# One transformer layer on one Trainium2 core: operand halves, k's pieces, norm scales and the first feed-forward weights made a step earlier at the joints between stages

## The chip, the cores and the metric

One core of one Trainium2 chip. TensorE (PE) multiplies, VectorE (DVE), ScalarE (ACT) and GpSimd (POOL) work on tiles in SBUF and PSUM, and SyncE (SP), POOL and ACT issue transfers. The metric is the time of one execution on the device in microseconds (us); lower is better.

## The reference

One layer on x of 1024 rows by 1024 columns, fp32, with three blocks, each between two RMS norms (`pre` before, `post` after, on the residual):

```python
h = swiglu(rmsnorm(x, ffn1_pre_g), wg1, wu1, wd1)        # 1024 -> 2816 -> 1024
x = x + 0.5 * rmsnorm(h, ffn1_post_g)
qkv = rmsnorm(x, mix_pre_g) @ w_qkv                      # 16 heads of 64
o_na  = neighbourhood_attention(heads 0..7)              # 2-D windows of a 16 x 64 grid
o_dil = dilated_mixture_attention(heads 8..15)           # windows (128,1) (512,4) (2048,16)
x = x + rmsnorm(concat(rmsnorm(o_na), rmsnorm(o_dil)) @ w_out, mix_post_g)
h = swiglu(rmsnorm(x, ffn2_pre_g), wg2, wu2, wd2)
x = x + 0.5 * rmsnorm(h, ffn2_post_g)
# swiglu(x, g, u, d) = (silu(x @ g) * (x @ u)) @ d
```

## The kernel before, in words

**Products.** Every fp32 operand is split into a high part (rounded to fp32r by ACT, names `whi`, `x`) and the remainder (DVE, `wlo`), and a product is three matmuls (`mm3`, L317 to L319). Gate, up, q, k and the down products go by the seven products of Strassen and Winograd over halves of 512 rows and columns. A left operand (`Operand`) therefore has quadrants A11, A12, A22 and sums S1 to S4; a right one (`PairGemm` for pairs such as gate and up of one block of 128 columns, or q and k) has B11, B22 and T1, T2.

**Operand.** The normed x comes in eight tiles of 128 rows. Tiles 0 to 3 are transposed on PE (`trp`, L157), split into A11 and A12, and a raw copy is saved to DRAM. Tile t from 4 on fetches the saved half of tile t-4 (`early_half`, L212, queue of POOL, shown as `x<-xn`) and forms the sums from it and from its own two transposes: `left_half`, `right_half`, with steps for S2, S1, S3 and at last S4 (`end`, L272), which the turns take one by one from a list. Where `c.deep` is 1 (the operands of q, k, v and of the second feed-forward; there `c.xn` is 0 and the norm is written in place) the fetched half has one place, tag `x1`.

**PairGemm.** `ahead` makes the A11 and A12 products of the first pairs (10 in the second feed-forward) while the operand's later tiles are still being made: a turn is two chains of four `mm3`, 24 matmuls. `start` fetches the first two weights (`graw`), `split_left(b)` splits weight b and fetches b+2. `run` then makes the rest of each pair: u2, v (L548, `v<-mmp,u`), c22 (L567), and in `last`, one turn later, c21 (L575, `c<-mmp,u`), the split of B22 and the fetch of the weights two pairs on. A sink takes the finished quarters: `GatePairs` for gate and up, `QKPairs` for q and k, which splits a piece (ACT L930, DVE L931, both named `qk`) and writes it to DRAM (L936 to L942; a strip is 128 by 8 by 64).

**Attention.** Eight dilated heads, then eight neighbourhood heads. Scores `sp` (L1051), their sums `sa` (L972), `q` and `g` sorted by residue on POOL (L961), probabilities transposed (`ptp`), copied (`pt`, L984), then `po`. Output goes to `og`. `GroupNorm` squares on ACT (L1213), makes 1/rms by a chain of small DVE operations (L131 to L143), scales `og` (L1220) and transposes it (L1231) as the operand of the out projection, whose turns `plan` fills with the next operand's steps: `fin.scale` and `rest` (L788), `U(t)` puts tile t, `G(t)` fetches a row block.

**Order.** `order` inside `ordered()` and the lists `todo`, `steps` and `sums` set which step is recorded in which turn; PE goes in the order in which the code is written, and a scheduler sorts the other engines' instructions by priority. Each engine and each queue runs in order. `nat_chain` products (`accp`) are the out projection's.

**Tail.** `Finish(...)` closes the second feed-forward: in `half` ACT squares a half of the product (L150) and DVE multiplies it by the gain in place (L750); `end` makes 1/rms (L128 to L143) and adds to the residual (L767).

## Time and profile before

| | us |
|---|---|
| median of 3 runs | 1929.8 (1928.88 to 1931.73) |
| the profiled execution | 1927.83 |
| its span, first to last instruction | 1926.0 |
| PE busy | 1851.6 (96%) |
| DVE busy | 1325.9 (69%) |
| ACT busy | 832.0 (43%) |
| POOL busy | 319.9 (17%) |
| mean granted clock of TensorE | 0.988 |

A row of a timeline has start and length in us, engine, line, operation, output from inputs, and in brackets the idle time of the engine just before and what ended it. A row of the waits has the engine's instruction, what it waited for, the total in us, how often, and the longest. The stages follow one another: first feed-forward to 690, q, k, v to 947 (the QK run from 840), attention to 1185, out projection to 1264, the second feed-forward's ahead phase to 1335, its run to 1700, the down products to 1915, tail to 1926.

### The profile page before, as it was taken

How to read it: one execution, taken by the hardware profiler on the slowest of the kernel's cores; microseconds unless marked ns; L12 is line 12 of the kernel's file. 1: busy time of each engine (PE TensorE's matmuls, PEld its weight loads, DVE VectorE, ACT ScalarE, POOL GpSimd, SP SyncE). 2: the span in 40 equal slices, each digit the busy share in tenths (PEclk: the TensorE clock that was granted, in tenths of full speed). 3: DMA queues.
4: the chain of work that ended last, by engine and by line, in shares of the span. 5: the costliest groups of instructions: out<-in, count | busy, mean ns of one | idle time of the engine just before them, and what ended most of it. 6: DMA issues, size and time to landing. Idle time of an engine off the chain costs nothing.

```text
span 1926.0 us, 25147 instructions
## 1 busy us (share of the span) xinstructions
PE 1851.6 (96%) x8904; PEld 1536.5 (80%) x8904; DVE 1325.9 (69%) x2233; ACT 832.0 (43%) x1491; POOL 319.9 (17%) x504
## 2 busy tenths in 40 slices
PE   7899999999999989998899998999999999999997
PEld 6787888888778867877799997877888888888886
DVE  6777776765565875556677765777788777654557
ACT  7422333333344555223488765455222333344332
POOL 2123211111030122122433100121111111110000
PEclk9999999999999999999999999999999999999999
DMA  7656565547886757556968540575456655476563
GB/s 270 211 169 207 204 225 211 195 164 248 295 306 216 269 187 257 193 178 221 299 224 259 170 142 23 190 280 186 158 192 238 216 193 210 159 267 216 200 227 136
DMA packets 169296, 404.95 MB, mean 210 GB/s; under 512 B 17793, under 2 KB 40225, under 8 KB 167122
## 3 DMA queue, kind: packets, MB, share of 16 engines
q1 hardware_dynamic: 121330, 242.66, 37.9%
q0 software_dynamic: 46832, 158.59, 22.9%
q10 hardware_dynamic: 1008, 2.10, 0.3%
q8 instruction: 70, 1.15, 0.2%
q14 instruction: 56, 0.46, 0.1%
HBM read 277.34 MB, written 130.99 MB: 212 GB/s over the span
## 4 chain that ended last, share of the span: by engine, by line
PE 47%; issue 27%; DMA 9%; DVE 9%; POOL 3%; ACT 3%; SPq 1%; DVEq 0%; POOLq 0%; ACTq 0%
PE mmp L319 9%; PE mmp L317 9%; PE mmp L318 9%; PE accp L318 4%; PE accp L319 4%; PE accp L317 4%; PE po L1072 2%; PE ptp L982 2%; DMA wraw<-in_wqk_dram 2%; PE po L1184 2%; DMA wraw<-in_wu_dram 1%; DVE pw L674 1%; DMA tsv<-tr 1%; PE sp L1051 1%; DVE wlo L414 1%
## 5 line engine op out<-in xcount | busy, mean ns | idle before, releaser
L317 PE MATMUL mmp<-x,whi 128*128 128x512 f32 (+1 forms) x1464 | 581.4, 397 | 19.4 <-DVE v L548 10.9
L319 PE MATMUL mmp<-x,wlo 128*128 128x512 f32 (+1 forms) x1464 | 577.5, 394 | 3.9 <-DVE wlo L414 3.9
L318 PE MATMUL mmp<-x,whi 128*128 128x512 f32 (+1 forms) x1464 | 575.7, 393 | 1.3 <-DVE x L240 0.8
L317 PEld LDWEIGHTS mmp<-x,whi 128*128 128x128 f32 x1464 | 278.2, 190 | 84.7 <-ACT whi L413 10.0
L319 PEld LDWEIGHTS mmp<-x,wlo 128*128 128x128 f32 x1464 | 277.9, 190 | 68.6 <-DVE wlo L414 5.9
L318 PEld LDWEIGHTS mmp<-x,whi 128*128 128x128 f32 x1464 | 278.3, 190 | 62.6 <-DVE x L240 1.1
L674 DVE TENSOR_TENSOR pw<-praw,pw 128x1024 fp32r<-128x1024 f32 (+1 forms) x181 | 199.7, 1148 | 115.7 <-ACT pw L673 115.3
L673 ACT CAST pw<-praw 128x1024 fp32r<-128x1024 f32 (+1 forms) x181 | 168.6, 982 | 208.3 <-PE accp L319 150.3
L318 PE MATMUL accp<-pw 128*128 128x512 f32 x600 | 234.4, 391 | 5.9 <-DVE pw L674 5.6
L317 PE MATMUL accp<-pw 128*128 128x512 f32 x600 | 234.8, 391 | 0.3 <-DVE hb L730 0.2
L319 PE MATMUL accp<-pw 128*128 128x512 f32 x600 | 233.6, 389 | 0.0
L413 ACT CAST whi<-wraw 128x1024 fp32r<-128x1024 f32 x129 | 135.3, 1051 | 219.1 <-PE mmp L318 184.5
L414 DVE TENSOR_TENSOR wlo<-wraw,whi 128x1024 fp32r<-128x1024 f32 x129 | 158.2, 1228 | 19.9 <-ACT whi L413 19.7
L318 PEld LDWEIGHTS accp<-pw 128*128 128x128 f32 x600 | 112.7, 188 | 31.6 <-DVE pw L674 9.0
L317 PEld LDWEIGHTS accp<-pw 128*128 128x128 f32 x600 | 112.7, 188 | 25.1 <-ACT pw L673 1.2
L319 PEld LDWEIGHTS accp<-pw 128*128 128x128 f32 x600 | 112.6, 188 | 23.3
L621 POOL DMA_DIRECT2D g<-sg x44 | 23.9, 544 | 471.1 <-DVE sg L614 296.4
L413 ACT CAST whi<-traw 128x512 fp32r<-128x512 f32 x52 | 32.4, 623 | 152.3 <-DVE traw L503 95.6
L502 DVE TENSOR_TENSOR wraw<-wraw 128x1024 f32<-128x1024 f32 x52 | 63.7, 1225 | 45.4 <-DMA wraw<-in_wqk_dram 26.2
L432 ACT COPY s<-mmp 128x512 f32<-128x512 f32 x52 | 30.6, 588 | 139.4 <-PE mmp L319 136.4
L575 DVE TENSOR_TENSOR c<-mmp,u 128x512 f32<-128x512 f32 x52 | 35.9, 690 | 76.9 <-PE mmp L319 76.8
L1184 PE MATMUL po<-vs,pt 128*128 128x128 f32 x352 | 50.3, 276 | 2.0 <-ACT pt L984 1.7
(278 smaller groups left out, 2761.1 us busy)
## 6 DMA issues: line engine op xcount, KB each, us to landing
praw<-g SPq DMA_DIRECT2D x70, 512.0 KB, 6.0
wraw<-in_wg_dram SPq DMA_DIRECT2D x44, 512.0 KB, 4.2
wraw<-in_wu_dram SPq DMA_DIRECT2D x44, 512.0 KB, 6.2
tr<-in_wd_dram SPq DMA_DIRECT2D x44, 512.0 KB, 6.5
g<-sg POOLq DMA_DIRECT2D x88, 256.0 KB, 4.1
ts<-tr POOLq DMA_DIRECT2D x22, 1024.0 KB, 4.8
praw<-ts SPq DMA_DIRECT2D x88, 256.0 KB, 4.3
praw<-in_wd_dram SPq DMA_DIRECT2D x66, 256.0 KB, 4.9
```

Source lines behind the costliest of these rows:

```text
L317: nc.tensor.matmul(out, ahi, bhi, start=start, stop=False, skip_group_check=go_on)
L318: nc.tensor.matmul(out, ahi, blo, start=False, stop=False, skip_group_check=go_on)
L319: nc.tensor.matmul(out, alo, bhi, start=False, stop=stop, skip_group_check=go_on)
L413: nc.scalar.copy(hi, raw)
L414: nc.vector.tensor_sub(lo, raw, hi.bitcast(F32))
L502: nc.vector.tensor_sub(r[:, 0:2], r[:, 1:3], r[:, 0:2])
L575: nc.vector.tensor_add(c21, d, u2)
L673: nc.scalar.copy(hi, raw[:, :m])
L674: nc.vector.tensor_sub(lo, raw[:, :m], hi.bitcast(F32))
L982: nc.tensor.transpose(ps[:, j, :], src[:, j * P:(j + 1) * P], c.ident)
L1072: nc.tensor.matmul(po[:, un * 2 + j], pt[:, 2 * j + t, :], rhs, start=t == 0, stop=t == 1)
L1184: nc.tensor.matmul(po[0][:, u], pt[0][:, j, :], vs[:, k0 + j, :], start=j == 0, stop=j == n - 1)
```

## The change

1. Operands with `c.xn` 0: the saved halves of tiles 5 and 7 are fetched as soon as tile 4's and tile 5's second transposes are recorded, into places of tag `x`; that of tile 6 at the end of tile 4, into `x1`.
2. `run` hands c22 to the sink right away (`third`); `QKPairs` puts k's second half there and no longer in `last`. The last pair's strips go by SP's queue.
3. End of attention: the squares of `most` and with them the norm of the first quad are recorded a turn sooner.
4. The second feed-forward's first weights are fetched at turn 6 of the out projection rather than 8, and weight 0 is split at its turn 10. Every third weight of the ahead phase, from 0 on, has a place of its own (`p0`), the others share two instead of three.
5. Tiles 6 and 7 of the second feed-forward's operand are put in turns 5 and 6 rather than 6 and 7.
6. In the tail the gain's product for the last four tiles goes to a tile `hm` of its own.

```diff
         self.parts[t] = deque(((A11, xn[:, :T]), (A12, xn[:, T:])))
-        if t >= 4:
+        if t == 4 or t > 4 and c.xn:
             self.early_half(t)
...
         c = self.c
-        x1 = self.half[t] = c.xp.tile([P, 2, 4, P], F32, tag="x1", name="x1", bufs=c.deep)
+        if t % 2 and not c.xn:
+            x1 = c.xp.tile([P, D], F32, tag="x", name="x1", bufs=c.xbufs).rearrange("p (i k x) -> p i k x", i=2, k=4)
+        else:
+            x1 = c.xp.tile([P, 2, 4, P], F32, tag="x1", name="x1", bufs=c.deep)
+        self.half[t] = x1
         c.nc.gpsimd.dma_start(x1, self.saved[t - 4].rearrange("p i (k x) -> p i k x", k=4))
...
             self.open -= 1
+            if t == 4 and not c.xn:
+                self.early_half(6)
         a22 = transposed(c, src)
+        if t in (4, 5) and not c.xn:
+            self.early_half(2 * t - 3)
         add(s1, a21, a22)
...
             nc.vector.tensor_add(c22, d, v)
+            self.sink.third(b, c22)
             sums()
...
 
+    def third(self, b, up):
+        pass
+
     def last(self, b, gate, up):
...
 
-    def __init__(self, c, src, dst, gain, op):
-        self.c, self.src, self.dst, self.gain, self.op = c, src, dst, gain, op
+    def __init__(self, c, src, dst, gain, op, last=False):
+        self.c, self.src, self.dst, self.gain, self.op, self.last = c, src, dst, gain, op, last
         self.ss = c.small.tile([P, 8, 2], F32, tag="fss", name="fss", bufs=1)
...
         sumsq(self.c, h, self.ss[:, t, g:g + 1])
-        self.c.nc.vector.tensor_mul(h, h, self.gain[:, g * T:(g + 1) * T])
+        to = h
+        if self.last and t >= 4 and g == 0:
+            to = self.part = self.c.xp.tile([P, T], F32, tag="hm", name="hm")
+        self.c.nc.vector.tensor_mul(to, h, self.gain[:, g * T:(g + 1) * T])
 
...
             sl = slice(g * T, g * T + T)
-            nc.vector.scalar_tensor_tensor(x[:, sl], h[:, sl], r, x[:, sl], op0=ALU.mult, op1=ALU.add)
+            nc.vector.scalar_tensor_tensor(x[:, sl], h[:, sl] if g else self.part, r, x[:, sl], op0=ALU.mult, op1=ALU.add)
             queue.dma_start(self.dst[t][:, sl], x[:, sl])
...
 
+    def third(self, b, k):
+        self.put(b, 1, 1, k)
+
     def last(self, b, q, k):
         self.put(b, 0, 1, q)
-        self.put(b, 1, 1, k)
 
...
                 dst = d[:, j].rearrange("p (s x) -> p s x", s=8)[:, :, h * 64:h * 64 + 64]
-                nc.gpsimd.dma_start(dst, e[:, j].bitcast(F32).rearrange("p (s x) -> p s x", s=8))
+                (nc.sync if h and b == 7 else nc.gpsimd).dma_start(dst, e[:, j].bitcast(F32).rearrange("p (s x) -> p s x", s=8))
         else:
...
             e = sub()
-            early_pools(e)
+            early_pools(e, 2 if pg.own else 3)
             if begin:
...
             c.pw, c.pr, c.ha, c.tj = pool("pw", 5, w), pool("pr", 4, w), pool("ha", 1, w), pool("tj", 1, m)
-            fin = Finish(c, src, dst, load_gain(c, post, "post"), None)
+            fin = Finish(c, src, dst, load_gain(c, post, "post"), None, pre is None)
             hs = {}
...
                     c.todo.append(lambda n=n, i=i: c.behind(lambda: n.squares(slice(0, 448), 0, (i, i + 1)), ACT))
+            c.tick()
         with ordered():
...
                     if (p, hd) == (NP - 1, 1):
-                        c.todo.extend([lambda: None, most])
+                        c.todo.append(most)
                     na_head(c, p, hd, og[0], vs, st, nb, next_ready, last if (p, hd) == (NP - 1, 1) else lambda q: None)
...
             pg = gate_pairs(3, op, a["wg2"], a["wu2"], 10)
+            pg.own = pool("p0", 1, prep, side="right")
             fin = Finish(c, x1, x2, p2, op)
...
                         c.behind(c.w.split, DVE, ACT)
-            plan(12, {0: [lambda: fin.scale(0, 4), A(0, 1)], 2: [A(2, 3)], 5: [U(0)], 6: [U(1)], 7: [G(4)],
-                      8: [lambda: queued(pg.start), G(5)], 9: [U(2)], 10: [U(3)], 11: [G(6)]})
+            plan(12, {0: [lambda: fin.scale(0, 4), A(0, 1)], 2: [A(2, 3)], 5: [U(0)], 6: [U(1), lambda: queued(pg.start)], 7: [G(4)],
+                      8: [G(5)], 9: [U(2)], 10: [U(3), lambda: pg.split_left(0)], 11: [G(6)]})
             for t in range(4):
...
             ffn(3, op, prep, pg, get2,
-                {0: [G(7), lambda: fin.scale(4, 4), A(4, 5)], 1: [A(6, 7)], 3: [U(4)], 4: [U(5)], 6: [U(6)], 7: [U(7)]},
+                {0: [G(7), lambda: fin.scale(4, 4), A(4, 5)], 1: [A(6, 7)], 3: [U(4)], 4: [U(5)], 5: [U(6)], 6: [U(7)]},
                 down_sums(a["wd2"], ts2), [], a["ffn2_post_g"], None, x2, o)
```

At the start of attention POOL's queue stood as follows before; `qk` are pieces of q and k on their way to DRAM, `st` and `q` the first head's operands, `g` its bias:

```order
251 L942 DMA qk_1_75<-qk 256x1x512
252 L961 COPY g<-g 128x384
253 L940 DMA qk_0_74<-qk 128x8x64 x2
254 L942 DMA qk_1_75<-qk 256x1x512
255 L942 DMA qk_1_77<-qk 256x1x512
256 L952 DMA st<-qk_0_78 128x1024
257 L961 COPY g<-g 128x384
258 L940 DMA qk_0_76<-qk 128x8x64 x2
259 L942 DMA qk_1_77<-qk 256x1x512
260 L961 COPY q<-st 128x1024
```

The same place after the change (L957, L959, L969, L978 are the former L940, L942, L952, L961):

```order
244 L957 DMA qk_0_72<-qk 128x8x64 x2
245 L959 DMA qk_1_75<-qk 256x1x512 x2
246 L978 COPY g<-g 128x384
247 L957 DMA qk_0_74<-qk 128x8x64 x2
248 L959 DMA qk_1_77<-qk 256x1x512 x2
249 L969 DMA st<-qk_0_78 128x1024
250 L978 COPY g<-g 128x384
251 L978 COPY q<-st 128x1024
```

The last pair's strips and pieces (`qk_0_76`, `qk_1_77`), which stood between the second `g` and `q`, are gone from between them: the strips to SP, the pieces of k ahead of `st` and that `g`.

On POOL, too, the second feed-forward's saved halves, `x_...<-xn_1` to `xn_3`, stood among the saves of the ahead phase's products (`s1d`, `sgd`), one per tile:

```order
330 L212 DMA x_11363<-xn_1_10688 128x1024
331 L487 DMA s1d<-s_11554 128x512
332 L604 DMA sgd<-sg 128x512
333 L487 DMA s1d<-s_11604 128x512
334 L212 DMA x_11439<-xn_2_10689 128x1024
335 L604 DMA sgd<-sg 128x512
336 L487 DMA s1d<-s_11656 128x512
337 L604 DMA sgd<-sg 128x512
338 L212 DMA x_11448<-xn_3_10690 128x1024
```

and now:

```order
318 L613 DMA sgd<-sg 128x512
319 L216 DMA x_11482<-xn_1_10688 128x1024
320 L495 DMA s1d<-s_11488 128x512
321 L613 DMA sgd<-sg 128x512
322 L216 DMA x_11531<-xn_2_10689 128x1024
323 L216 DMA x_11551<-xn_3_10690 128x1024
324 L495 DMA s1d<-s_11557 128x512
325 L613 DMA sgd<-sg 128x512
```

The fetches of the last two tiles now follow that of tile 5 after two saves, next to each other (L216, L495, L613 are the former L212, L487, L604).

On DVE the first of the second feed-forward's `wlo<-graw` stood in pair with the second before:

```order
1497 L240 TENSOR_TENSOR x_10686<-raw,x_10685 128x4x128
1498 L134 TENSOR_SCALAR y<-v 128x4
1499 L135 TENSOR_SCALAR y<-y 128x4
1500 L141 TENSOR_TENSOR e<-y,v 128x4
1501 L414 TENSOR_TENSOR wlo<-graw,whi 128x1024 x2
1502 L142 TENSOR_TENSOR e<-e,y 128x4
1503 L143 SCALAR_TENSOR_TENSOR y<-e,y 128x4
```

and stands now in the out projection, among the small operations of the pre-norm's scale (L133 to L143) and the products by the gain (L1790):

```order
1454 L133 TENSOR_SCALAR v<-ss 128x2
1455 L1790 TENSOR_TENSOR hs<-accp,gain 128x512
1456 L134 TENSOR_SCALAR y<-v 128x2
1457 L1790 TENSOR_TENSOR hs<-accp,gain 128x512
1458 L135 TENSOR_SCALAR y<-y 128x2
1459 L422 TENSOR_TENSOR wlo<-graw,whi 128x1024
1460 L141 TENSOR_TENSOR e<-y,v 128x2
1461 L142 TENSOR_TENSOR e<-e,y 128x2
```


The first weight's low part (L422 is the former L414) moved out of the phase that needs it into the stage ahead; the second stays where the pair was.

## The prediction

> **What bounds the kernel now.** I read the page's busy shares first, then the waits of TensorE (PE) summed by releaser, then the windows and the timelines around the longest of these waits. The first fence has the page's busy line and then windows (span, length, busy time of PE, PEld, DVE, ACT, POOL, granted clock, DMA share, GB/s).
>
> ```profile
> PE 1851.6 (96%) x8904; PEld 1536.5 (80%) x8904; DVE 1325.9 (69%) x2233; ACT 832.0 (43%) x1491; POOL 319.9 (17%) x504
> 720.00:730.00 10.00, 6.91 (x24) 5.33 (x23) 4.46 (x6) 3.05 (x5) 1.72 (x3) 0.83 0.63 215
> 855.00:865.00 10.00, 7.21 (x33) 5.67 (x32) 7.74 (x10) 4.14 (x5) 4.61 (x7) 1.00 0.81 222
> 950.00:960.00 10.00, 7.80 (x41) 7.32 (x41) 4.57 (x24) 7.44 (x23) 6.09 (x5) 0.66 1.06 344
> 1185.00:1195.00 10.00, 7.51 (x32) 5.64 (x32) 7.57 (x32) 3.67 (x16) 0.00 (x0) 0.83 0.00 0
> 1264.00:1335.00 71.00, 64.87 (x280) 50.40 (x278) 56.08 (x99) 41.84 (x70) 15.63 (x29) 0.95 0.69 238
> 1265.00:1275.00 10.00, 7.78 (x20) 5.73 (x21) 8.32 (x20) 4.82 (x8) 2.09 (x4) 0.66 0.67 226
> 1334.00:1344.00 10.00, 9.66 (x34) 7.55 (x35) 6.65 (x9) 3.29 (x5) 0.54 (x1) 0.83 0.91 322
> 1335.00:1700.00 365.00, 365.00 (x1584) 298.24 (x1584) 271.77 (x342) 114.11 (x150) 47.27 (x83) 1.00 0.56 194
> ```
>
> PE is busy 96% of the span, and in the long run of the second feed-forward (1335 to 1700) all of it: 365.00 us for 1584 matmuls is 0.230 us each, so a turn of 24 matmuls there lasts 5.5 us. No edit removes a matmul, so only time in which PE stands still or runs at a lower clock can be won. The joints between stages have both. A window of 10 us at clock 0.83 loses 10 x 0.17 = 1.7 us, one at 0.66 loses 3.4.
>
> The waits of PE by releaser (total, times, longest) name the places:
>
> ```profile
> PE mmp L317 <- DVE v L548: 10.9, 7, 2.8
> PE mmp L317 <- ACT whi L413: 4.4, 2, 2.3
> PE mmp L319 <- DVE wlo L414: 3.9, 3, 3.1
> PE sp L1051 <- DVE sa L972: 2.9, 1, 2.9
> PE trp L1231 <- DVE og L1220: 2.5, 1, 2.5
> PE sp L1051 <- POOL q L961: 1.7, 1, 1.7
> ```
>
> **The change, part by part.**
>
> *Operand of q, k, v (term a).* The fetch of a tile's saved half (L212) waited for the one place of x1, which comes free at the previous tile's last subtraction (L272). For tiles 5 and 7 it now goes to a place of x right behind the transposes, for tile 6 right behind tile 4's end. DVE around the wait of 3.1:
>
> ```profile
> 717.88 0.69 DVE L278 TENSOR_TENSOR s<-s,x 128x512 f32<-128x512 f32 x1 [0.82 <-DMA x<-xn]
> 722.10 2.35 DVE L414 TENSOR_TENSOR wlo<-graw,whi 128x1024 fp32r<-128x1024 f32 x2
> 723.37 0.50 PE L319 MATMUL mmp<-x,wlo 128*128 128x512 f32 x1 [3.09 <-DVE wlo L414]
> ```
>
> DVE stood 0.82 for that fetch, and the wlo that PE needs stands behind all of tile 5's subtractions. In the new order one wlo goes ahead of two of them (2 x 0.69) and the 0.82 is gone: 2.2 of the 3.09. Ends: 0.8 (the 0.82 alone) and 3.1. New issues on POOL cost nothing on the path: POOL is 17% busy.
>
> *k's second half a step sooner (term b).* In seven turns of the QK run PE waits for v, 10.9 in all.
>
> ```profile
> 859.82 1.08 DVE L931 TENSOR_TENSOR qk<-c,qk 128x512 fp32r<-128x512 f32 x1 [0.33 <-ACT qk L930]
> 870.08 1.23 DVE L502 TENSOR_TENSOR wraw<-wraw 128x1024 f32<-128x1024 f32 x1 [6.64 <-DMA wraw<-in_wqk_dram]
> ```
>
> At 859.82 k's subtraction stands ahead of v; it moves behind it, 0.33 + 1.08 = 1.4 sooner. But the next turn starts with weights whose landing DVE already awaits for 6.64, so that turn gives most of it back. I take 1.0; ends 0 and 2.
>
> *Start of attention (term c).* The last pair's subtraction for k and its DMAs stood between PE's last matmul and the first scores; the strips go to SP.
>
> ```profile
> 947.98 1.08 DVE L931 TENSOR_TENSOR qk<-c,qk 128x512 fp32r<-128x512 f32 x1 [1.25 <-ACT qk L930]
> 948.98 0.68 DVE L931 TENSOR_TENSOR qk<-qk 128x512 fp32r<-128x512 f32 x1
> 948.76 0.91 POOL L940 DMA_DIRECT2D qk<-qk  x1 [0.27 <-ACT qk L930]
> 949.96 0.89 POOL L940 DMA_DIRECT2D qk<-qk  x1 [0.28 <-DVE qk L931]
> 950.84 0.70 POOL L942 DMA_DIRECT2D qk<-qk  x1
> 951.42 2.13 POOL L961 CAST q<-st 128x1024 fp32r<-128x1024 f32 x1
> ```
>
> One subtraction goes ahead of the others, about 1.0 off the wait of 2.9 for the scores' sums; the other (948.98) stays. POOL's cast of q stood behind three issues (0.91 + 0.89 + 0.70 with waits between, 2.7): without them it ends sooner than PE needs it, and the wait of 1.7 goes. Sum 2.7; ends 1.0 (q then waits for the landing of st) and 4.6 (both waits whole). What SP gets is two issues ahead of the first loads of v, needed only after the scores.
>
> *End of attention (term d).* The chain of twelve small operations that makes the scale, from the second row to the third, ran behind the last og; it now stands ahead, in the 2.28 in which DVE idled.
>
> ```profile
> 1184.10 0.42 DVE L1192 TENSOR_TENSOR og<-po,rd 128x256 f32<-128x256 f32 x1 [2.28 <-PE po L1184]
> 1184.44 0.15 DVE L131 TENSOR_TENSOR v<-gss 128x4 f32<-128x4 f32 x1
> 1187.02 2.08 DVE L1220 SCALAR_TENSOR_TENSOR og<-og,y,gd 128x512 f32<-128x512 f32 x3
> 1175.44 0.56 ACT L1213 ACTIVATE junk<-og 128x448 bf16<-128x448 f32 x1
> ```
>
> 1187.02 - 1184.44 = 2.6 less before the transpose: the whole wait of 2.5. Against it, squares such as that of 0.56 on ACT now stand among the copies that PE awaits; I charge one. 2.0; ends 0 (four of them are paid) and 2.5.
>
> *First weights of the second feed-forward (term e).* ACT and DVE made them after the out projection, where nothing covered them:
>
> ```profile
> 1265.92 2.01 ACT L413 CAST whi<-graw 128x1024 fp32r<-128x1024 f32 x2
> 1267.16 2.36 DVE L414 TENSOR_TENSOR wlo<-graw,whi 128x1024 fp32r<-128x1024 f32 x2
> ```
>
> The first split now stands some 25 us earlier, beside the out projection's matmuls. What goes is the wait for whi, 2.3, and 0.2 more for wlo: 2.5. If that cover is gone (DVE is dense there) the piece costs 1.0 + 1.2 where it is put, and 0.3 is left: ends 0.3 and 2.5. The two new places of weights keep a rotation of three, so no later weight is fetched later.
>
> *Tiles 6 and 7 a turn sooner, halves fetched early (term f).*
>
> ```profile
> 1307.90 0.69 DVE L278 TENSOR_TENSOR s<-s,x 128x512 f32<-128x512 f32 x1 [2.82 <-DMA x<-xn]
> 1331.70 1.22 DVE L502 TENSOR_TENSOR wraw<-wraw 128x1024 f32<-128x1024 f32 x1
> L269 DVE TENSOR_TENSOR x<-s,x 128x512 fp32r<-128x512 f32 x16 | 10.7, 687 | 1.5 <-ACT x L268 1.4
> L414 DVE TENSOR_TENSOR wlo<-graw,whi 128x1024 fp32r<-128x1024 f32 x10 | 12.1, 1222 | 1.4 <-ACT whi L413 1.4
> ```
>
> At the phase's end PE waits 2.1 (4.4 less 2.3) for whi, since DVE comes to the run's first weights only at 1331.70; 0.6 more is left of the waits for wlo (3.9 - 3.1 - 0.2). DVE's 2.82 for the fetch goes, and the tiles come 5.5 sooner, so DVE is there before PE. 2.5; ends 0 and 2.7.
>
> *Tail (term g).* Four tiles run in a chain on DVE; the gain's product waits for ACT's square, which reads the same tile:
>
> ```profile
> 1901.33 0.69 DVE L733 TENSOR_TENSOR hb<-accp,hb 128x512 f32<-128x512 f32 x1 [2.81 <-PE accp L319]
> 1915.18 0.39 PE L319 MATMUL accp<-pw 128*128 128x512 f32 x1
> 1917.50 0.69 DVE L733 TENSOR_TENSOR hb<-accp,hb 128x512 f32<-128x512 f32 x1
> 1919.03 0.69 DVE L750 TENSOR_TENSOR hb<-hb,gain 128x512 f32<-128x512 f32 x1 [0.85 <-ACT junk L150]
> ```
>
> From 1901.33 to 1917.50 is three tiles, 5.39 each, against PE's 4.75: the first add starts as its matmuls end, and the last matmul is out at 1915.57, 14.2 later. With a tile of its own the product fills the 0.85, and the scale starts when ACT's sum is in, 0.6 sooner per tile. 5.39 - 0.6 = 4.8, about PE's own pace: the last tile starts 1.8 sooner and ends 0.6 sooner still, 2.4. Ends 0.6 and 2.5.
>
> *Clock (term h).* Windows at 0.83 or 0.66 stand behind five of the waits: q, k, v 1.7, start of attention 3.4, its end 1.7, first weights 3.4, end of the phase 1.7, in all 11.9. The tie isn't strict: 855 to 865 holds the longest wait for v, 2.8, and shows 1.00. I count half of the four whose wait goes (8.5), so 4.2, and nothing at the start of attention, where a wait of 1.9 stays; ends 0 and 11.9. [...]
>
> Sum: 2.2 + 1.0 + 2.7 + 2.0 + 2.5 + 2.5 + 2.4 + 4.2 = 19.5. The profiled execution took 1927.83 (span 1926.0 and 1.83 around it), which gives 1908.3; the median of the runs lies 1.97 above it, so the forecast is 1910.
>
> **The rivals.** [...]
>
> *The feed-forward's joint gives nothing* (e = f = 0): the split is paid in the out projection, and DVE, now fed four tiles in four turns, is as late at the end as before. Left are 2.2 + 1.0 + 2.7 + 2.0 + 2.4 = 10.3 and half of 3.4 of clock (terms a and d), 12.0: 1918.
>
> *Other waits in the same places:* landings end each joint instead of the queues; only g's 2.4 stay, 1927. Against it speaks that in a, d, e, g the last releaser is an engine.
>
> *DVE becomes the bound and the kernel is slower.* A tile takes nine operations of 0.687 (L276, L278, L279, L272 and five of L269), 6.2, and the turn's weight 1.22: 7.4 against PE's 5.5. With tiles 4 to 7 in consecutive turns DVE falls back 1.9 in each; if wlo is queued behind the tiles, PE waits four times 1.9, 7.6, and each wait draws 1.7 of clock: 14.4 lost, against 10.3 won elsewhere: 1929.8 + 4.1 = 1934. For it: DVE is busy 56.08 of 71 us there. Against: 15 us are idle, the 2.82 goes, and wlo is ordered ahead of some tile steps. It decides once the losses of the phase pass what the other joints save, 10.3.
>
> **How the numbers follow.** Forecast 0.46, clock as it is 0.22, joint without gain 0.18, other waits 0.06, DVE bound 0.08. The range takes in the first three with their bounds: all low ends and no clock would be 2.7 off, all high ends 31.8 off, both unlikely, so 1901 to 1925. Some 0.2% (3.9 us) is what a measurement of this kernel can tell from no change: faster 0.86, same 0.06, slower 0.08.
>
> **What would show it.** Right: the waits named og L1220, POOL q and ACT whi L413 missing from PE's list; wlo at the q, k, v joint under 0.6; the last hb add at about 0.2 behind PE's last matmul; clock 1.00 in the windows behind. Wrong: waits of PE for wlo or x between the feed-forward's turns, or a second low window there; DVE waiting for graw or x1 landings; L548 waits still at 10.

## The result

The changed kernel ran at 1917.24 us (median of 4, 1916.26 to 1917.54) beside 1930.76 for the kernel before: ratio 0.9947, interval 0.993 to 0.9964. Run twice more beside before, it came to 0.9940 (0.9928 to 0.9952) and 0.9941 (0.9925 to 0.9956). So it is 0.5 to 0.6% faster, 11 to 13.5 us by the medians; the forecast was 20.

The page after, and the waits of TensorE (total, times, longest) over the whole span, as they answer to those before:

```profile
span 1915.8 us, 25139 instructions
PE 1846.7 (96%) x8904; PEld 1535.6 (80%) x8904; DVE 1328.6 (69%) x2233; ACT 832.6 (43%) x1491; POOL 318.2 (17%) x502
PE mmp L325 <- DVE v L556: 7.2, 4, 3.4
PE trp L157 <- DVE x L204: 5.8, 1, 5.8
PE sp L1068 <- DVE sa L989: 3.5, 1, 3.5
PE accp L325 <- DVE hb L742: 1.9, 1, 1.9
PE mmp L327 <- DVE wlo L422: 0.9, 2, 0.5
PE trp L1248 <- DVE og L1237: 0.7, 1, 0.7
```

(L325 to L327 are the former L317 to L319, L421 and L422 the former L413 and L414, L273 the former L269.) The waits that an edit aimed at are down or gone: og from 2.5 to 0.7, q from POOL gone, wlo at q, k, v from 3.1 to 0.4 (the other 0.5 of its row lies in the second feed-forward). That for sa has grown from 2.9 to 3.5, and one for hb is new.

To see where the time went I matched one DVE instruction per stage in the traces. Each number is how much longer a stage took than in the profiled execution of before (us; minus is faster). The stages end at: the add of the thirteenth hb (679.4 in before), the first k (834.4), the last k (943.3), the first neighbourhood head's og (1080.7), the last hs (1265.1), the run's last c (1705.6), the last pass's first hb (1884.5), the end.

| kernel | first feed-forward | q, k, v | QK run | attention start | its end, out projection | 2nd feed-forward | down | tail | all |
|---|---|---|---|---|---|---|---|---|---|
| forecast, with half of the clock | 0 | -3.1 | -1.0 | -2.7 | -2.9 | -7.6 | 0 | -2.4 | -19.5 |
| changed | +1.8 | -3.6 | +0.1 | -1.9 | -4.4 | -3.4 | +1.8 | -0.5 | -10.3 |
| again | +2.1 | -3.1 | +0.9 | -2.0 | -4.4 | -1.8 | +0.4 | -2.0 | -9.9 |
| again2 | +0.2 | -2.6 | -1.3 | -2.0 | -4.5 | -3.7 | +0.6 | -2.1 | -15.4 |
| no_halves | +2.8 | -0.7 | +2.9 | -1.1 | -3.1 | +1.1 | +1.2 | -2.0 | +1.0 |
| no_turn67 | -0.3 | -2.3 | -0.4 | -1.6 | -4.4 | -3.9 | +0.1 | -2.1 | -14.9 |
| no_first | -0.1 | -3.8 | +1.0 | -1.2 | -4.3 | -3.1 | +0.5 | -2.0 | -13.1 |
| no_qk | +0.9 | -4.8 | +0.5 | -1.0 | -4.4 | -3.5 | +0.3 | -2.4 | -14.6 |
| no_most | +1.7 | -1.3 | +1.3 | -1.8 | -1.8 | -2.0 | +1.9 | -0.6 | -2.5 |
| no_tail | +1.0 | -3.9 | -0.7 | -2.0 | -4.5 | -3.3 | +2.0 | +0.4 | -11.0 |
| sp7 | +0.6 | -2.6 | -1.0 | -2.0 | -4.4 | -4.0 | +1.3 | -2.1 | -14.2 |
| order_fix | -0.0 | -3.6 | -1.4 | -2.0 | -4.4 | -5.0 | +0.4 | -2.0 | -18.0 |
| order2 | +0.6 | -2.8 | +3.1 | -1.9 | -3.1 | -4.0 | +0.2 | -1.1 | -8.9 |
| q_on_act | -0.2 | -4.1 | +1.1 | -2.5 | -4.5 | -1.8 | +0.1 | -2.0 | -13.9 |
| joined | -1.4 | -2.7 | -0.7 | -2.7 | -3.1 | -4.8 | -0.2 | -2.1 | -17.7 |
| joined2 | -0.7 | -2.8 | +2.3 | -2.7 | -4.4 | -6.5 | -0.1 | -2.1 | -17.1 |
| joined3 | +3.2 | -3.4 | -0.7 | -2.5 | -3.1 | -5.3 | -0.2 | -2.1 | -14.0 |
| warm | +6.7 | -0.8 | +1.6 | -1.8 | -4.5 | -2.0 | -0.8 | -1.7 | -3.4 |
| warm_joined2 | +5.4 | -3.1 | +4.0 | -2.6 | -3.1 | -6.5 | -0.7 | -2.0 | -8.6 |
| pick | +2.7 | -3.1 | -1.0 | -0.4 | -4.4 | -6.1 | +0.0 | -2.5 | -14.8 |

The first feed-forward and the QK run scatter by 4 to 5 us from one execution to the next, in kernels that are alike there; the start of attention repeats within about 1. The tail is at about -2; changed and no_most show less because a stretch of half clock in the last pass cost them 1.5, order2 because its end came 1.0 later, and no_tail has the edit undone. The largest gap against the forecast is the second feed-forward: 7.6 was expected, 1.8 to 3.7 came in three executions.

TensorE's clock splits these three. The traces record stretches of half clock, 3.4 us or a multiple long (3.41 and 6.83 at 0.50 in that of the changed kernel, from 876.25 and 947.93). Changed and again2 have none in this phase (-3.4, -3.7), again has one of 3.4 (-1.8). Five more kernels have the same code there: no_tail and no_qk without a stretch are at -3.3 and -3.5, no_most, q_on_act and warm with one at -1.8 to -2.0. One stretch is therefore worth about 1.6 in this column, and runs are best compared with others that have as many.

Waits of TensorE in that phase alone, before (1258 to 1340) and after (1250 to 1332):

```profile
PE mmp L317 <- ACT whi L413: 4.4, 2, 2.3
PE mmp L317 <- ACT s L432: 0.8, 1, 0.8
PE mmp L319 <- DVE wlo L414: 0.8, 2, 0.6
```

```profile
PE trp L157 <- DVE x L273: 2.6, 2, 1.8
PE mmp L325 <- ACT whi L421: 1.5, 1, 1.5
PE mmp L325 <- ACT raw L238: 1.4, 1, 1.4
PE trp L157 <- ACT s L260: 1.3, 1, 1.3
PE mmp L327 <- DVE wlo L422: 0.5, 1, 0.5
```

Before they come to 6.0, after to 7.3. Not one microsecond of waiting was won there: the first weights' wait passed to the copy that frees a PSUM bank (raw, 1.4), and three waits of the transposes are new. What was won is clock. In before 1264 to 1335 had 0.95; after, the same phase has:

```profile
1256.00:1326.00 70.00, 63.75 (x289) 50.35 (x287) 56.94 (x102) 41.70 (x69) 16.18 (x30) 1.00 0.72 256
```

The two low windows of before there (0.66 from 1265, 0.83 from 1334) had lost 3.4 and 1.7, together 5.1; 5.1 of clock won and 1.3 more waiting make 3.8, about the 3.4 measured.

Why the transposes wait stands on DVE and POOL (timelines of the changed kernel):

```profile
1269.84 0.55 POOL L613 DMA_DIRECT2D sgd<-sg  x1 [2.46 <-ACT sg L609]
1270.37 0.55 POOL L495 DMA_DIRECT2D s1d<-s  x1
1270.91 0.54 POOL L804 DMA_DIRECT2D x<-x  x1
1280.90 1.28 DVE L204 SCALAR_TENSOR_TENSOR x<-x,y,gain 128x1024 f32<-128x1024 f32 x1 [2.75 <-DMA x<-x]
1284.16 1.23 DVE L510 TENSOR_TENSOR wraw<-wraw 128x1024 f32<-128x1024 f32 x1 [0.84 <-DMA wraw<-in_wu_dram]
1285.30 0.68 DVE L284 TENSOR_TENSOR s<-s,trp 128x512 f32<-128x512 f32 x1
1324.93 0.62 ACT L421 CAST whi<-traw 128x512 fp32r<-128x512 f32 x1 [1.96 <-PE mmp L326]
```

Row block 7 is stored to DRAM and then normalised in place (L204), so DVE has to see the store read. The changed order put that store on POOL behind a product's `sgd`, which waits for ACT. It was issued 3.2 after DVE had made the block and landed 9.4 after its issue had ended, and DVE stood 2.75. Then it stood for L510, a sum of the second pair's weights, taken far ahead of its use. Tile 4 begins only behind both. And at the run's start ACT took the second pair's T2 (`traw`), whose place TensorE was still reading, ahead of the first pair's T1, for which TensorE then waited.

### The profile page after: what moved, and what is told of

It reads as the page before. It is cut to its first block, busy times and chain, and to the rows that moved or that the text cites. A ratio compares the mean times of both kernels' runs of the same rounds, so it can differ in the third digit from the quotient of the medians.

```text
span 1915.8 us, 25139 instructions
## 1 busy us (share of the span) xinstructions
PE 1846.7 (96%) x8904; PEld 1535.6 (80%) x8904; DVE 1328.6 (69%) x2233; ACT 832.6 (43%) x1491; POOL 318.2 (17%) x502
## 5 line engine op out<-in xcount | busy, mean ns | idle before, releaser
L325 PE MATMUL mmp<-x,whi 128*128 128x512 f32 (+1 forms) x1464 | 580.3, 396 | 15.9 <-DVE v L556 7.2
L327 PE MATMUL mmp<-x,wlo 128*128 128x512 f32 (+1 forms) x1464 | 576.9, 394 | 0.9 <-DVE wlo L422 0.9
L325 PEld LDWEIGHTS mmp<-x,whi 128*128 128x128 f32 x1464 | 278.0, 190 | 79.9 <-issue 5.1
L327 PEld LDWEIGHTS mmp<-x,wlo 128*128 128x128 f32 x1464 | 277.7, 190 | 64.2 <-DVE wlo L422 2.2
L325 PE MATMUL accp<-pw 128*128 128x512 f32 x600 | 235.6, 393 | 2.4 <-DVE hb L742 1.9
L421 ACT CAST whi<-wraw 128x1024 fp32r<-128x1024 f32 x129 | 135.3, 1051 | 231.6 <-PE mmp L326 211.5
L327 PE MATMUL accp<-pw 128*128 128x512 f32 x600 | 234.4, 391 | 0.0
L422 DVE TENSOR_TENSOR wlo<-wraw,whi 128x1024 fp32r<-128x1024 f32 x129 | 158.2, 1229 | 19.9 <-ACT whi L421 19.8
L325 PEld LDWEIGHTS accp<-pw 128*128 128x128 f32 x600 | 113.0, 188 | 27.2 <-issue 2.3
L327 PEld LDWEIGHTS accp<-pw 128*128 128x128 f32 x600 | 113.1, 189 | 23.5
L421 ACT CAST whi<-traw 128x512 fp32r<-128x512 f32 x52 | 32.3, 622 | 141.2 <-DVE traw L511 76.0
L510 DVE TENSOR_TENSOR wraw<-wraw 128x1024 f32<-128x1024 f32 x52 | 63.7, 1224 | 35.5 <-DMA wraw<-in_wqk_dram 25.3
L575 DVE TENSOR_TENSOR c<-mmp,v 128x512 f32<-128x512 f32 x52 | 35.9, 690 | 25.1 <-PE mmp L327 24.6
```

What stands on the lines that cost most here:

```text
L325: nc.tensor.matmul(out, ahi, bhi, start=start, stop=False, skip_group_check=go_on)
L327: nc.tensor.matmul(out, alo, bhi, start=False, stop=stop, skip_group_check=go_on)
L421: nc.scalar.copy(hi, raw)
L422: nc.vector.tensor_sub(lo, raw, hi.bitcast(F32))
L510: nc.vector.tensor_sub(r[:, 0:2], r[:, 1:3], r[:, 0:2])
L575: nc.vector.tensor_add(c22, d, v)
```

## The experiments

**The parts undone, one at a time.** The change's own kernel once more:

> The changed kernel once more, unaltered. If the profiled execution of it was typical, the ratio to before is 0.993 to 0.996 again, the second feed-forward's waits of transposes (1.4, 2.0 and 0.9) stand in the new trace at the same places, and the wait of 1.9 for hb in the down products either stands again (then the change causes it) or is gone (then it was one execution's landing).

0.9940 of before. The transposes' waits stood at the same places (1.28, 1.83 and 0.75 of idle time, some 0.17 less than the expectation's way of counting from matmul to matmul). The wait for hb was 0.5. It comes to 1.4 to 2.2 in no_halves, no_most, no_tail and sp7 as well, where, as in changed, DVE stood 7.6 to 8.8 for a row block of the residual (5.3 in before); the down products took 1.2 to 2.0 longer in these five. In again2, where DVE stood 8.0, it is 0.8. So it comes and goes with a landing that varies between executions; whether the change has a part in it is not shown.

```diff
-                {... 5: [U(6)], 6: [U(7)]},
+                {... 6: [U(6)], 7: [U(7)]},
```

> The changed kernel with tiles 6 and 7 of the second feed-forward put in turns 6 and 7 again, all else kept. If DVE is what sets the ahead phase (four tiles in a row at 7.4 against PE's 5.5), the waits of transposes shrink by about 2 to 3 and as much comes back at the phase's end: no change within 1.5 against the changed kernel. If putting them sooner was worth the 2.5 of the forecast, this is 2.5 slower than the changed kernel. If it costs, this is 2 to 3 faster.

0.9929 (0.9916 to 0.9942), the phase at -3.9. The waits of transposes go, those of 0.4 and 2.0 ahead of the run come back, and the phase's waits sum to 5.8, not 7.3. Putting the tiles a turn sooner is worth nothing; if anything it costs, since this execution has one stretch of half clock in the phase and the changed order with one is at -1.8 to -2.0.

```diff
-            pg.own = pool("p0", 1, prep, side="right")
-            ... 6: [U(1), lambda: queued(pg.start)] ... 10: [U(3), lambda: pg.split_left(0)]
+            ... 6: [U(1)] ... 8: [lambda: queued(pg.start), G(5)] ... 10: [U(3)]
```

> The changed kernel with the first weights fetched and split where they were before (and the three shared places). If the split in the out projection was worth the forecast 2.5, this is 2.5 slower, and up to 6 with the low clock behind it. If the wait at the phase's start only passes to the copy that frees a PSUM bank (1.4 in the changed kernel's trace), 1 slower. If DVE sets the phase, the start is later by 1 to 2 and the transposes' waits shrink by as much: no change.

0.9951 (0.9937 to 0.9964), the phase at -3.1, inside the scatter of the changed kernel (-1.8 to -3.7). The start waits 2.3 and 0.7 again; the transposes' waits fall from 3.9 to 3.0 and the run's start has none. The phase's waits sum to 6.0 instead of 7.3: fetching and splitting the first weight sooner saved no waiting.

```diff
-        if t == 4 or t > 4 and c.xn:
+        if t >= 4:
             self.early_half(t)
...
-        if t in (4, 5) and not c.xn:
-            self.early_half(2 * t - 3)
```

> The changed kernel with every saved half fetched at its own tile into the one place, as before. At q, k and v the wait for wlo is back at 3.1 with a low clock behind it: 3 slower there. In the second feed-forward tiles 6 and 7 come a turn sooner and each half still waits for the place: if the early fetch is what lets DVE go on, the transposes' waits grow by 2 or more; if DVE's work sets the phase, by less than 1. In all 3 to 6 slower.

0.9994 (0.9982 to 1.0007): 1.9 to 2.9 of q, k, v are lost and 3 to 5 in the second feed-forward, where one transpose now waits 4.1 for DVE (the 2.3 in the second row is the wait at q, k, v, come back):

```profile
PE trp L157 <- DVE x L270: 5.7, 3, 4.1
PE mmp L320 <- DVE wlo L415: 3.0, 3, 2.3
```

With four tiles in a row the early fetch is what keeps the phase from being slower than before. The rest lies for the most part in the QK run (+2.9), which scatters and was not edited here.

```diff
-            self.sink.third(b, c22)
...
     def last(self, b, q, k):
         self.put(b, 0, 1, q)
+        self.put(b, 1, 1, k)
...
-                (nc.sync if h and b == 7 else nc.gpsimd).dma_start(...)
+                nc.gpsimd.dma_start(...)
```

> The changed kernel with k's second half put in last, after q's, as before, and all strips on POOL. If terms b and c were as forecast (1.0 and 2.7), 3.7 slower. If DVE's stand for POOL's cast gives back most of c and the QK run goes by its weights' landings, 1 to 2 slower, with the wait for q of 1.7 back and the last subtraction at 0.69.

0.9931 (0.9914 to 0.9948), no slower than the changed kernel. The start of attention loses 0.9, the QK run nothing that can be told from its scatter. The last subtraction is back at 0.68, the wait for sa at 2.6, and that for q is 1.2, not 1.7.

```diff
-            c.tick()
         with ordered():
...
-                        c.todo.append(most)
+                        c.todo.extend([lambda: None, most])
```

> The changed kernel with the squares and the first quad's scale recorded where they were. If the whole of what the traces show between the first neighbourhood head and the out projection's end is due to it, 4.4 slower: 2.5 of wait and 1.7 of low clock. If the clock there is not tied to the wait, 2.5.

0.9951 (0.9932 to 0.9969). The wait of 2.5 for og is back and the stage takes 2.6 longer: the wait's own size, with no low stretch behind it in this execution.

```diff
-            fin = Finish(c, src, dst, load_gain(c, post, "post"), None, pre is None)
+            fin = Finish(c, src, dst, load_gain(c, post, "post"), None)
```

> The changed kernel with the gain's product in the tail written in place again. The period of the last four tiles is 5.39 again rather than 4.79, and the end comes 2.0 to 2.4 later after the last pass's first add: 2 slower than the changed kernel. If PE or the last write to DRAM set the end, nothing changes.

0.9961 (0.9949 to 0.9973); the tail takes 2.4 longer (+0.4 against -2.0). Against before the edit is worth 2.0: from the first add of the last four tiles to the end it is 22.65 in the changed kernel and 24.70 in before. The adds (the first and the last of four, changed, then without the edit) follow one another every 4.79 and every 5.39:

```profile
1893.10 0.69 DVE L745 TENSOR_TENSOR hb<-accp,hb 128x512 f32<-128x512 f32 x1 [2.81 <-PE accp L327]
1907.47 0.68 DVE L745 TENSOR_TENSOR hb<-accp,hb 128x512 f32<-128x512 f32 x1
```

```profile
1889.96 0.69 DVE L745 TENSOR_TENSOR hb<-accp,hb 128x512 f32<-128x512 f32 x1 [2.81 <-PE accp L327]
1906.13 0.69 DVE L745 TENSOR_TENSOR hb<-accp,hb 128x512 f32<-128x512 f32 x1
```

**The second feed-forward's waits taken away.** First the store:

```diff
-            nc.gpsimd.dma_start(self.dst[t], x)
+            (nc.sync if t == 7 and getattr(self, "sp", False) else nc.gpsimd).dma_start(self.dst[t], x)
```

> The changed kernel with one transfer moved: the store of row block 7 before the second feed-forward goes by SP's queue, not POOL's, where it stands behind the saves of two products. In the changed kernel DVE stood 2.75 for that store (it normalises the same tile in place). If DVE sets the phase, this is 2 to 2.75 faster than the changed kernel, and the transposes' waits (4.3 together) fall by as much. If something else sets it (banks, weights), the store's wait goes and the time stays.

0.9935 (0.9923 to 0.9947), the phase at -4.0 without a stretch of half clock, 0.3 to 0.7 better than the four executions that have none either (-3.3 to -3.7). The store's wait went, and DVE stood longer for the second pair's weights in its place:

```profile
1283.92 1.23 DVE L510 TENSOR_TENSOR wraw<-wraw 128x1024 f32<-128x1024 f32 x1 [4.72 <-DMA wraw<-in_wu_dram]
```

Next, ACT's order at the run's start:

```diff
                 direct()
-                second()
+                if b or self.own is None:
+                    second()
+                else:
+                    c.behind(second, ACT)
```

> The changed kernel with one order held: at the start of the second feed-forward's run, ACT splits the first pair's T1 and B22 before the next pair's T2. In the changed kernel's trace ACT took the next pair's T2 first and stood 1.96 for PE to be done with the place that it writes, and PE then waited 1.5 for T1's high part and 0.7 for the low one. If that order is what ends the phase there, those two waits go: 2.2 faster than the changed kernel. If DVE's lateness sets it, T1's low part is late all the same and under 0.7 is won.

0.9946 (0.9927 to 0.9965), the phase at -5.0, 1.3 to 1.7 better than those four, and again without a stretch. The wait for T1's high part is gone; that for its low part is now 1.5, since DVE's own order is the same:

```profile
1322.90 0.50 PE L327 MATMUL mmp<-x,wlo 128*128 128x512 f32 x1 [1.46 <-DVE wlo L422]
```

With `direct` and `second` both queued behind, on DVE and ACT (`c.behind(lambda: (direct(), second()), DVE, ACT)`):

> The changed kernel with the second pair's first weight sums and splits queued behind the first pair's splits on both DVE and ACT. In the changed kernel DVE takes the second pair's first sum 32 us before it can use it, right ahead of tile 4, and stands for its weights there; and the two engines take the second pair's T2 ahead of the first pair's T1. With only ACT's order held, PE's wait at the start of the run shrank from 2.3 to 1.6 and stood on DVE. If this order ends the phase, the wait is now under 0.4: 2 faster than the changed kernel, measured from the last sums of the out projection to the run's last pair. If DVE's work sets the phase, the wait stays over 1.

0.9957 (0.9942 to 0.9971), the phase at -4.0. I had expected under 0.4 at the run's start; it is 2.6. Queued like that, L510 and the sum u stand ahead of T1's low part. The wait moved and grew.

Four parts together (turns 6 and 7, store on SP, ACT's order, q on ACT):

> The changed kernel with four things together: tiles 6 and 7 put in turns 6 and 7 as before, the store of row block 7 on SP, the order of the splits on ACT held, q of the first head on ACT. If the causes are separate, 3 (turns) + 0.5 to 2.5 (store) + 2.2 (order) + 1.5 (q) add up: 6 to 8 faster than the changed kernel, about 1908 where before is 1928. If they hide each other (one DVE behind all in the feed-forward's phase), 3 to 5.

0.9929 (0.9916 to 0.9942), the phase at -4.8. DVE, rid of the store, stands 6.0 for the second pair's weights, with tile 4 queued behind:

```profile
1276.80 1.22 DVE L422 TENSOR_TENSOR wlo<-graw,whi 128x1024 fp32r<-128x1024 f32 x1
1284.06 1.23 DVE L510 TENSOR_TENSOR wraw<-wraw 128x1024 f32<-128x1024 f32 x1 [6.04 <-DMA wraw<-in_wu_dram]
1285.20 0.68 DVE L284 TENSOR_TENSOR s<-s,trp 128x512 f32<-128x512 f32 x1
```

The same four parts, but with both engines' order held as in order2:

> As joined before (tiles 6 and 7 in turns 6 and 7, store on SP, q on ACT), with both engines' order held. There DVE stood 6.0 for the second pair's weights ahead of tile 4, and PE 2.6 for a transpose and 1.6 at the run's start. If both are that order, both go: 4 faster than joined, up to 3.4 of low clock besides. If only the second goes, 1.6.

0.9934 (0.9922 to 0.9946), the phase at -6.5, the best of all, though with one stretch of half clock. No transpose waits any more; what is left is T1's order and the bank:

```profile
PE mmp L327 <- DVE wlo L422: 2.6, 1, 2.6
PE mmp L325 <- ACT raw L238: 1.4, 1, 1.4
```

The same again, with the turns as the change has them:

> As joined2, with tiles 6 and 7 in turns 5 and 6, as the change has them. If DVE, rid of its two waits, keeps up with a tile in each turn, this is as fast as joined2 or up to 1 faster; if four tiles in a row are more than it can do (7.4 against 5.5 each), PE waits for transposes again, 2 to 4 in all, and this is that much slower than joined2.

0.9933 (0.9921 to 0.9946), the phase at -5.3: with DVE rid of both stands, four tiles in a row cost one wait of a transpose of 0.8, not 2 to 4. So the prediction's 7.4 of DVE's work per turn against PE's 5.5 is a small part; DVE's two stands are the large one.

**The start of attention.**

```diff
-            c.behind(lambda: qs.append(q_by_residue(c, nc.gpsimd.tensor_copy, loaded[0][1])), POOL)
+            c.behind(lambda: qs.append(q_by_residue(c, nc.scalar.copy, loaded[0][1])), ACT)
```

> The changed kernel with the first head's q sorted by ACT rather than POOL. In the changed kernel DVE's last subtraction before the first scores (128 x 512, elsewhere 0.69) lasted 2.16, and ended 0.55 after POOL's cast of q. If the two share a way to SBUF and DVE stood for POOL, the subtraction is back under 1.1 and PE's wait for sa falls from 3.5 to about 2.0: 1.5 faster, up to 3 with less low clock. If DVE was slow for another reason, it stays at 2.16 and nothing is won, or ACT's own copies come 1 later.

0.9936 (0.9923 to 0.9949). DVE's last subtraction and POOL's cast of q in the changed kernel, then that subtraction here:

```profile
945.85 2.10 POOL L978 CAST q<-st 128x1024 fp32r<-128x1024 f32 x1
946.34 2.16 DVE L948 TENSOR_TENSOR qk<-qk 128x512 fp32r<-128x512 f32 x1 [1.40 <-ACT qk L947]
```

```profile
944.92 0.69 DVE L948 TENSOR_TENSOR qk<-qk 128x512 fp32r<-128x512 f32 x1 [1.40 <-ACT qk L947]
```

The subtraction lasted 2.16 while POOL's cast ran and 0.69 without it, as expected. PE's wait for sa falls from 3.5 to 2.0, but the stage gains only 0.5 to 0.6: the strided cast takes ACT 2.04 (944.80 to 946.84) and the exponentials come behind it.

**The clock.** Extra matmuls that nobody reads, meant to fill three waits:

```diff
+            if (self.pi, hd, part, quad, un) == (0, 0, 0, 1, 1):
+                warm = c.psm.tile([P, T], F32, tag="mm", name="warm")
+                for _ in range(24):
+                    nc.tensor.matmul(warm[:, :256], st[:, 0, :P], st[:, 1, :256], start=True, stop=True)
...
+        warm = self.x[A11][0] if t == 4 and self.which < 2 else None
+        c.nc.scalar.copy(s[:, 0], transposed(c, src, warm))   # 20 matmuls of 512 columns
```

> The changed kernel with extra matmuls, whose results nobody reads, in three places where PE stands for another engine: 20 of 512 columns ahead of tile 4's transposes of the first two operands (waits of 4.9 and 5.8), 24 of 256 columns ahead of the first scores' second group (wait of 3.5). If a standing PE draws the low clock, the stretches behind these three places (3.4 or 6.8 each at half speed) go, and the kernel is 3.4 to 8 faster with more work in it. If the low clock comes from something else, they stay and the time is the same, or up to 2 slower where the extra matmuls run past the wait.

0.9956 (0.994 to 0.9972), not faster. But at two of the three places the clock did what was expected if a standing PE draws the stretches. Windows at q, k, v and at the start of attention, of the changed kernel and then of this one:

```profile
700.00:715.00 15.00, 9.20 (x40) 7.50 (x40) 13.67 (x37) 8.08 (x16) 4.88 (x9) 0.77 0.64 222
945.00:960.00 15.00, 11.49 (x79) 11.29 (x77) 9.77 (x36) 10.89 (x34) 6.10 (x7) 0.77 0.99 329
```

```profile
706.00:721.00 15.00, 13.28 (x67) 10.67 (x66) 13.93 (x37) 8.88 (x16) 4.76 (x9) 1.00 0.67 228
953.00:968.00 15.00, 12.69 (x99) 11.45 (x98) 9.58 (x33) 10.81 (x34) 6.69 (x6) 1.00 1.05 348
```

Both low stretches are gone, and both stages take no less time (q, k, v -0.8, attention start -1.8). In the first, DVE is busy 13.9 of 15 us and sets the pace. From tile 4's first transposes to the wait for wlo, the traces of the changed order take 16.7 to 17.8 with 6.8 us of half clock, 16.7 with 3.4 (no_qk), 17.3 with none (warm and warm_joined2), and 18.0 with 10.2 (no_most). Up to 6.8 us of half clock cost nothing there. At the start of attention they cost little: with 3.4 joined, joined3 and q_on_act are at -2.5 to -2.7, and joined2 with none is at -2.7; with q on POOL, executions with 6.8 are at -1.1 to -1.9 and those with 3.4 at -1.9 to -2.0.

At the third place, in the first feed-forward, the extra matmuls ran ahead of the wait, not in it: tile 4's transposes came 4.1 later (62.28 against 58.20), their wait was 4.7 against 4.9, and the stretch of 6.8 behind it stayed.

> The extra matmuls of warm on top of joined2. If the parts add up, as much faster than joined2 (0.9934 of before) as warm is than the changed kernel: 1905 to 1909 where before is 1927. If low stretches only move to the next wait of over 2 us (there are three in the QK run), half of that.

0.9937 (0.992 to 0.9954), no better than joined2. Both windows are at 1.00 again; joined2 had no stretch at the start of attention to begin with, and the one at q, k, v had cost it nothing.

**The pick.** Without k's earlier piece and the earlier turns, with the store on SP and ACT's order:

> The changed kernel without k's earlier piece and the strips on SP, with tiles 6 and 7 in turns 6 and 7, the store of row block 7 on SP, and ACT's order of the splits held. If those two edits were worth nothing and the mended orders 1 to 3 each, 0.990 to 0.993 of before and 2 to 6 faster than the changed kernel beside it. If the waits only pass on, the same as the changed kernel.

> The changed kernel, unaltered, for comparison on this chip: 0.993 to 0.9955 of before.

On the same chip 0.9923 (0.9908 to 0.9938) against 0.9941 (0.9925 to 0.9956), 1912.96 against 1916.36. It has the lowest ratio of all, but the intervals overlap, as do those of joined, no_turn67 and no_qk: that it is some 3 us better than the changed kernel is likely, not shown.

## Why the prediction was right or wrong

The direction and the range held (1917.2 within 1901 to 1925); the size was 20 where 11 to 13.5 was measured. By its terms:

- **a, q, k, v: the wait right, the sum partly by luck.** 3.1 with its clock, 2.6 to 3.6 measured; no_halves loses 1.9 to 2.9 of it. The wait fell by 2.7, not 2.2, and the clock added nothing: half clock lasts 6.8 in sum there in both traces.
- **b, k's piece in the QK run: too large.** 1.0 expected, about 0 within a scatter of 4; PE's waits for v sum to less (7.2 against 10.9, with 2.1 more booked as another wait), but DVE's own waits for the weights' landings hardly moved (24.4 before, 23.4 after, from 840 to 947), and these the forecast's own row of 6.64 had shown.
- **c, start of attention: mis-sized,** 2.7 against 1.9, of which undoing it loses 0.9 to 1.6. The wait for q went. The price missed was that POOL's cast, come sooner, lies beside DVE's last subtraction and holds it 1.5: the subtraction lasted 2.16 and ended at 948.50, 0.55 after the cast (947.95), and q_on_act, which has the cast on ACT, brought it back to 0.69. By what the one holds the other is not shown.
- **d, end of attention: mechanism right, sized low.** 4.4 against 2.9: the wait of 2.6 whole (no_most), no square paid, and before's low stretch gone.
- **e and f, the second feed-forward: the step that failed.** 5.0 less waiting was forecast and 1.3 more came (6.0 to 7.3); "DVE is there before PE" did not hold. I took away the wait of 2.82 for the saved half and did not ask what DVE's queue would stand for next. It was the store of row block 7, which the new order of POOL put behind a product's save, then the weights of L510. Before's trace had the second one already. Its groups in 1264 to 1335 (busy time, mean ns | idle time ahead of it) show 3.1 of DVE's waiting for the same weights:

```profile
L502 DVE TENSOR_TENSOR wraw<-wraw 128x1024 f32<-128x1024 f32 x2 | 2.4, 1222 | 3.1 <-DMA wraw<-in_wu_dram 3.1
```

  With both stands taken away and the turns as before (joined2) the waits come to 4.0 and the phase to 6.5. What the change did win in the phase is clock, 5.1 before and none after, and that belongs to h. The rival "the feed-forward's joint gives nothing" had half of this mechanism (DVE as late as before), and at 1918 the time.
- **g, tail: right,** 2.4 expected, 2.4 measured by no_tail and 2.0 against before. In the changed kernel's first profiled execution the column shows only 0.5, since a stretch of half clock in the last pass took 1.5.
- **h, clock: right as a cause, wrong place by place.** That a standing PE draws the low stretches is shown by warm at two places (0.77 to 1.00 in both windows). But I priced all of them as if PE set the pace. At q, k, v and the start of attention it does not, and little or nothing is to be had. Where it does, a stretch of 3.4 costs nearly the whole 1.7: 1.3 to the out projection's end (-4.4, and -3.1 in the five executions whose unchanged wait of 1.9 near 1190 drew one), 1.5 in the last pass, about 1.6 in the second feed-forward. There the change won more than the half I had counted: 1.7 behind og and 5.1 in the feed-forward's phase. That is partly luck, for the sum was made on one execution of before, and the same wait draws a stretch in one execution and none in the next.
- The rest is scatter, as far as these runs show: the first feed-forward and the down products, where nothing was edited, took 0.8 to 3.6 longer than in the one execution of before that the sum was made against. That one (1927.83) lay below all four runs measured beside the changed kernel (1928.88 to 1933.08).

The rival of a slower kernel by DVE alone was wrong in its price: the cost of four tiles in a row, DVE's stands removed, is one wait of 0.8. But no_halves shows how near it was: without the early fetch the same order is as slow as before.

## What to carry to other kernels

DVE's queue hid the next wait behind the present one: with the store's 2.75 gone, DVE stood 4.72 for the second pair's weights at the same place (sp7). So before a wait is booked as won, go down that engine's queue and write the arrival time of each operand beside it, stores that a tile's reuse depends on included. A step moved sooner lands beside other work; see what runs or queues beside it there, as POOL's cast of q beside a subtraction that then took 2.16 and not 0.69. And price a slow clock only in stages where the engine that slows sets the pace (up to 6.8 us of half clock cost nothing at q, k, v, while 3.4 us cost about 1.6 in the second feed-forward), and compare executions that have as many slow stretches there.

## What was not expected of the hardware

In the traces of before and of the changed kernel TensorE's clock fell to half for 3.41 or 6.83 us at a time (between 20 and 1895 us) behind waits, several of them shorter than 3.4 us: in before 3.41 behind those of 2.45 for og (1187.91) and 2.42 for v (877.91), in the changed kernel 3.41 behind one of 1.91 for hb (1875.54). Behind others it did not fall: in before those of 2.79 and 2.31 for v (861.65 and 895.54); and the unchanged wait of 1.9 near 1190 has a stretch behind it in 5 of 19 executions (the rows of -3.1 above). The length of the stretch behind the same wait varies from one execution to the next (3.4 behind that of 5.5 at the start of q, k, v in before, 6.8 behind its 5.8 in the changed kernel).

Those two traces have 16 such stretches. In the 3.41 us just ahead of each PE was busy 0 to 44%. In joined the wait of 1.9 lies in the 3.41 us ahead of a stretch, 1.55 of them busy, and half clock followed (the 0.50 of the second row):

```profile
1185.31:1188.72 3.41, 1.55 (x10) 1.06 (x9) 2.69 (x6) 1.21 (x4) 0.00 (x0) 1.00 0.02 5
1188.72:1192.13 3.41, 3.41 (x13) 2.71 (x12) 1.67 (x4) 1.35 (x4) 0.00 (x0) 0.50 0.00 0
```

In the changed kernel no stretch stands behind that wait; the 3.42 us from 1190.27 were 1.91 busy, and the clock stayed at 1.00:

```profile
1190.27:1193.69 3.42, 1.91 (x13) 1.73 (x14) 2.01 (x6) 1.46 (x5) 0.00 (x0) 1.00 0.00 0
1193.69:1197.10 3.41, 3.37 (x18) 2.56 (x17) 2.03 (x5) 1.38 (x4) 1.64 (x4) 1.00 0.05 13
```

What decides whether a stretch follows stays open.
